# One core, a diffusion block with expert retrieval: left-over dots gather into the ring, the fourth tile's projection moves behind three heads, the first tile's norm moves to the last stage's end

## The chip, the core and the metric

The kernel runs on one core of a Trainium2 chip. Its engines are TensorE (PE in the profile; PEld is its weight load), VectorE (DVE), ScalarE (ACT), GpSimd (POOL) and the queue of SyncE (SP), which here only issues DMAs. GpSimd issues the indirect DMAs (gathers); all transfers run on the same 16 DMA engines. The metric is the device time of one execution in microseconds; lower is better. The median of three runs of the kernel before is 1616.89 us.

## What is computed

One layer of a hybrid block: a mixer (a gated recurrence and a gated linear attention, with an output projection `w_out`), then a retrieval of experts, then a final norm. For this change the second half matters. Each of 512 latent tokens has 8 heads; each head picks 16 of 16,384 experts, so 128 experts a token:

```python
act = jax.nn.gelu(jnp.einsum("td,tkd->tk", xb, u_tab[eb]), approximate=False) * wb
return jnp.einsum("tk,tkd->td", act, v_tab[eb])
...
x = x + mod_l[:, 5] * _peer(u_l, peer_w_q[l], peer_keys[l], peer_u[l], peer_v[l])
return _rmsnorm(x, final_norm_g)
```

`u_tab` and `v_tab` are 16,384 x 1024 floats each. A token needs the dot product of its vector with 128 rows of U, a gelu, and the weighted sum of 128 rows of V.

## The kernel before

The 512 tokens are four tiles of 128: `t0`, `t1` (the list GT) and `d0`, `d1` (the list DT). The two pairs go two ways.

**Gathered tiles (t0, t1).** For each of the 128 experts of a token a gather brings 128 rows of U, one for each token of the tile (128 x 1024 floats), and VectorE forms the dot products of the rows (`u_start` issues the gather, `u_fin` is the dot, L924). After every 16 dots (a head) ScalarE takes the gelu and VectorE multiplies by the weights (`u_done`, L932 and L936). Then 128 gathers of V rows are summed with these weights: for t1 by VectorE (`v_row`, L982), for t0 by TensorE, 128 matmul pairs into the PSUM tile `yv` (`v_pairs`, L973).

**Dense tiles (d0, d1).** The whole U table is streamed in 128 blocks `b` of 128 experts: `d_scores` (L1030) multiplies each block with both tiles, gives 128x256 scores and keeps them, after a gelu, in the three parts of A. The chosen experts' weights are multiplied in by `w_hot`, `w_mm` and `w_mul`. Then the whole V table is streamed (`v_load`, four buffers): `v_split` cuts a block of V and of A into a high and a low part (`vh`, `gh` on ScalarE, `vl`, `gl` on VectorE, L1078 and L1077) and `d_out` (L1090) multiplies gh vh, gh vl and gl vh into `ya`; every sixth block is multiplied unsplit. Blocks 126 and 127 are multiplied at the end, tile by tile, each followed by that tile's `finish`.

**Stages.** (1) The front, to about 402 us: mixer, then for each tile the output projection with its norm (`prep_mm`, 32 matmuls), its transposes (`prep_t`), and the queries and scores of the heads (`q_mm`, `s_mm`). (2) The scores stage, to 910 us: `d_scores` on TensorE; beside it VectorE picks the experts (`select`) and does dots. (3) The weights stage, to 1120 us: `w_*` for the dense tiles and V rows of t0 on TensorE, with 14 dots of t1. (4) The last stage, to the end: `v_split` and `d_out`; beside them the remaining dots of t1 and its 128 V rows (the generator `rest`), then the norms.

**What sets the order.** In stages 2 to 4 the engines run in the order in which the code emits (`manual_schedule`). In the front and stage 2 two generators, `pe_list` and `dve_list`, are merged by two clocks of planned microseconds; a dot of t0 or t1 is put in (`row_u`) whenever VectorE's clock has reached `due`, which then grows by PACE. `done` is a set of marks: "sel" once both dense tiles are picked (before block 100), "end" at block 121, after which no dots are put in, "u" after block 127. In stage 4, after each `d_out(b)`, `rest` is advanced until `want` of its steps are done.

**Buffers.** `ring` has four buffers of 128x1024 floats. Before "sel" every third dot gathers into another tag, `rz`. After "u" a dot gathers into `rw`, which has the tag u_d, two buffers; `vl` has the same tag:

```python
if "u" in done:
    g = B.tile([128, D], F32, name="rw", tag="u_d", bufs=2)
elif "sel" not in done and k % 3 == 2:
    g = zs.tile([128, D], F32, name="rz", bufs=2)
else:
    g = ring()
...
vl = B.tile([128, D], F32R, name="vl", tag="u_d", bufs=2)
```

`finish(t, yt)` is a tile's gated sum and final norm: `fin_rows` loads the gate row and the norm's weights into two ring buffers, `fin_x` the tile's x, and a fourth buffer is scratch. For t0 it stands at the start of stage 4 and reads `yv` in PSUM; t1's stands after block 126.

Of the kernel before, what the change touches and what calls it, by code (L numbers as in the profile page):

```python
# [9 lines left out]
F32 = mybir.dt.float32  # L10
# [10 lines left out]
D = 1024  # L21
# [26 lines left out]
def tile_kernel(ctx, tc, x, cx, pos, ada_w, cols, rows, consts, w_in, wgate, w_g, w_out, w_q, keys_t,  # L48
                peer_u, peer_v, peer_ut, out):
    nc = tc.nc  # L50
    V, S, G, PE, SY = nc.vector, nc.scalar, nc.gpsimd, nc.tensor, nc.sync
# [246 lines left out]
    w = load_in(2464)  # L298
# [325 lines left out]
    for n, k in enumerate((0, 1, 2, 3, 4, 5, 6, 7)):  # L624
        tag, nb = (("acc", 1) if n < 1 else ("wraw", 3) if n < 4 else ("whi", 2) if n < 6 else ("wlo", 2))
        w = wst.tile([128, D], F32, name="wo", tag=tag, bufs=nb)
# [3 lines left out]
    t0, t1 = GT  # L630
    d0, d1 = DT
# [38 lines left out]
    def ring(shape=(128, D), dt=F32):  # L670
        return B.tile(list(shape), dt, name="ring", tag="ring", bufs=RING)
# [10 lines left out]
    def prep_mm(t):  # L682
        xt, pt = xin[t]
        V.tensor_add(xt, xt, pt)
        for n in range(2):
            p = bank("pw")
            for k in range(KD):
                PE.matmul(p, mix_k(k)[:, t * 128:(t + 1) * 128], wo[k][:, n * 512:(n + 1) * 512],
                          start=(k == 0), stop=(k == KD - 1))
            V.tensor_mul(pt[:, n * 512:(n + 1) * 512], p, gate_mix[:, n * 512:(n + 1) * 512])  # L690
        V.tensor_add(xt, xt, pt)
        SY.dma_start(x1_d[t * 128:(t + 1) * 128, :], xt)
        ss = kb.tile([128, 1], F32, name="ss1", bufs=2)
        S.activation(pt, xt, AF.Square, accum_out=ss)
        r = rstd_of(kb, ss, 1, 1.0 / D)
        V.tensor_scalar(pt, xt, r[:, 0:1], None, op0=OP.mult)
# [4 lines left out]
    def prep_t(t):  # L701
        pt = xin[t][1]
        ut = [tok_u(t, k) for k in range(KD)]
        for h in range(2):
            p = bank("pt")
            for j in range(4):
                PE.transpose(p[:, j * 128:(j + 1) * 128], pt[:, (h * 4 + j) * 128:(h * 4 + j + 1) * 128], ident)
            for j in range(4):
                k = h * 4 + j
                if j % 2:  # L710
                    S.activation(ut[k], p[:, j * 128:(j + 1) * 128], AF.Identity,
                                 scale=a2[:, k:k + 1], bias=b2[:, k:k + 1])
                else:
                    V.tensor_scalar(ut[k], p[:, j * 128:(j + 1) * 128], a2[:, k:k + 1], b2[:, k:k + 1],
                                    op0=OP.mult, op1=OP.add)

    def prep_n(t):
        u_n[t] = B.tile([128, D], F32, name=f"u_n{t}")
        for h in range(2):
            p = bank("pu")  # L720
            for j in range(4):
                PE.transpose(p[:, j * 128:(j + 1) * 128], tok_u(t, h * 4 + j), ident)
            S.copy(u_n[t][:, h * 512:(h + 1) * 512], p)
# [129 lines left out]
    L = {}  # L853
# [58 lines left out]
        return g  # L912

    def u_start(t, k):
        if "u" in done:
            g = B.tile([128, D], F32, name="rw", tag="u_d", bufs=2)
        elif "sel" not in done and k % 3 == 2:
            g = zs.tile([128, D], F32, name="rz", bufs=2)
        else:
            g = ring()  # L920
        return t, k, gather(peer_u, sel_i[t][:, k:k + 1], g)
# [33 lines left out]
    yv = []  # L955
# [30 lines left out]
    def fin_rows():  # L986
        fin["gp"] = ring()
        fin["fn"] = ring()
        SY.dma_start(fin["gp"], gp_d)
        SY.dma_start(fin["fn"], row(2))  # L990

    def fin_x(t, g):
        fin[t] = g
        SY.dma_start(g, x1_d[t * 128:(t + 1) * 128, :])

    def finish(t, yt):
        xt, tm = fin[t], ring()
        ss = kb.tile([128, 2], F32, name="ss2", bufs=2)
        for n in range(2):
            c = slice(n * 512, (n + 1) * 512)  # L1000
            V.tensor_mul(tm[:, c], yt(n), fin["gp"][:, c])  # L1001
            V.tensor_add(xt[:, c], xt[:, c], tm[:, c])  # L1002
            S.activation(tm[:, c], xt[:, c], AF.Square, accum_out=ss[:, n:n + 1])  # L1003
        s1 = kb.tile([128, 1], F32, name="ss1", bufs=2)
        V.tensor_add(s1, ss[:, 0:1], ss[:, 1:2])
        r = rstd_of(kb, s1, 1, 1.0 / D)
        for n in range(2):
            c = slice(n * 512, (n + 1) * 512)
            V.scalar_tensor_tensor(xt[:, c], xt[:, c], r[:, 0:1], fin["fn"][:, c], op0=OP.mult, op1=OP.mult)  # L1009
            SY.dma_start(out[t * 128:(t + 1) * 128, c], xt[:, c])  # L1010
# [100 lines left out]
    done = set()  # L1111
# [7 lines left out]
    def pe_list():  # L1119
        prep_mm(t0)  # L1120
        prep_mm(t1)
        yield 28
        prep_mm(d0)
        prep_t(t0)
        prep_t(t1)
        yield 16
        between = {1: lambda: (prep_n(t0), prep_mm(d1)), 3: lambda: prep_t(d0), 4: lambda: prep_n(t1),
                   5: lambda: prep_t(d1)}
        last = None
        for h in range(NH):  # L1130
            for a in (h * 2 + 4, h * 2 + 5):
                if a < 16:
                    wq_load(a)
            q = q_mm(GT, h)
            if last:
                s_mm(*last)
            last = q
            if h in between:
                between[h]()
            yield 22.5 if h == 1 else 8.2  # L1140
        s_mm(*last)
        open_l()
        done.add("l")
        seq = [("u", 0), ("u", 1)]
        for h in range(NH):
            seq += [("w", 2 * h), ("w", 2 * h + 1)] + [("u", 4 * h + 2 + i) for i in range(4)]
        seq += [("u", b) for b in range(34, 128)]
        for n in range(3):
            u_load(*seq[n])
        last = None  # L1150
        region.enter_context(tc.manual_schedule(engines={ET.Activation, ET.PE, ET.DVE, ET.Pool}))
        for n, (kind, b) in enumerate(seq):
            if n + 3 < len(seq):
                u_load(*seq[n + 3])
            if kind == "w":
                if b % 2:
                    if last:
                        s_mm(*last)
                    last = q_mm(DT, b // 2)
                    yield 8.1  # L1160
                continue
            if b == A_PARTS[1]:
                open_a(1)
            if b == A_PARTS[2]:
                while not all(("turn", t) in done for t in DT):
                    yield None
                done.add("sel")
                open_a(2)
            d_scores(b)
            if last and b == 34:  # L1170
                s_mm(*last)
                last = None
            yield 3.45
            if b == 121:
                done.add("end")
        done.add("u")
        flush(True)
        region.close()
# [31 lines left out]
        while "end" not in done:  # L1210
            yield None

    PACE = 2.4
    due = 70.
    ET = mybir.EngineType
    region = ExitStack()
    clock = [0.0, 52.0]
    streams = [pe_list(), dve_list()]
    while streams[0] or streams[1]:
        if "l" in done and "u" not in done:  # L1220
            flush()
        if "end" not in done and clock[1] >= due and clock[1] <= clock[0] + 4 and row_u():
            clock[1] += 1.32
            due = max(due + PACE, clock[1] - 6)
            continue
        i = 0 if streams[0] and (clock[0] <= clock[1] or not streams[1]) else 1
        c = next(streams[i], "end")
        if c == "end":
            streams[i] = None
        elif c is None:  # L1230
            clock[i] = clock[1 - i] + 0.1
        else:
            clock[i] += c
# [25 lines left out]
    if "usage" in globals():  # L1259
        usage("end")  # L1260
    L["y"] = B.tile([128, D], F32, name="y", tag="u_n0")
    fin_rows()
    fin_x(t0, ring())
    finish(t0, lambda n: yv[0][:, n, :])

    def rest():
        for h in range(NH):
# [3 lines left out]
            for _ in range(TOPK):  # L1271
                v_row(t1, left[t1]["v"].pop(0))
                yield

    n_g = len(left[t1]["u"]) + NSEL
    gath = rest()
    k = 0
    with tc.manual_schedule(engines=PIN):
        v_split(0)
        for b in range(128):  # L1280
            if b < 127:
                v_split(b + 1)
            if b + 4 < 128:
                v_load(b + 4)
            elif b < 127:
                fin_x((t1, d0, d1)[b - 124], slot([128, D], "xf"))
            if b < 126:
                d_out(b)
            want = min(n_g, n_g * (b + 1) // 124)
            while k < want:  # L1290
                next(gath, None)
                k += 1
            if b == 124:
                next(gath, None)
                fin_rows()
            if b == 126:
                finish(t1, lambda n: L["y"][:, n * 512:(n + 1) * 512])
        for t in DT:
            for b in (126, 127):
                d_out(b, (t,))  # L1300
            finish(t, lambda n: ya[t][:, n, :])
# [67 lines left out]
```

## Time and profile before

| | |
|---|---|
| runs shown (us) | 1609.41, 1616.89, 1619.64; median 1616.89 |
| profiled execution (us) | 1608.13, of which the span 1606.4 |
| mean granted clock of TensorE | 0.975 of full speed |
| busy, share of the span | PE 93%, PEld 69%, DVE 74%, ACT 33%, POOL 39% |
| matmuls | 6668 |
| stages (us from the span's start) | front to 402, scores to 910, weights to 1120, last to the end |
| moved by DMA | 484.28 MB, mean 301 GB/s |

The busy shares are means over four stages with different limits, so what a change is worth is read stage by stage. A row of a timeline gives start, duration, engine, line, operation, and in brackets the idle time of that engine just before, with what ended it. A busy TensorE is not TensorE at its peak, since matmuls overlap and their ends are modelled.

### The profile page before, as it was taken

The page shows a single profiled execution, that of the slowest core. Times are in us where ns is not written, and L with a number is a line of the kernel's source. Part 1 is how long each engine was busy: PE and PEld are TensorE (multiplying, and loading weights), DVE is VectorE, ACT ScalarE, POOL GpSimd, SP SyncE. Part 2 cuts the span into 40 slices and gives each one's busy share as a digit, 9 for nine tenths or more (in the row PEclk, how much of TensorE's full clock was granted, in tenths as well). Part 3 has the DMA queues.
Part 4 walks back from the last instruction along what each step waited for, and adds up shares of the span by engine and source line. Part 5 has one row for each costly group of instructions (what it writes and reads, how often), then busy time and mean ns, then how long its engine had stood idle before and what let it go on. Part 6 is the DMA issues. An engine that isn't in the chain of part 4 may idle for free. (4 is left out here: it accounts for less than half of the span.)

```text
span 1606.4 us, 20273 instructions
## 1 busy us (share of the span) xinstructions
PE 1486.4 (93%) x6668; PEld 1103.9 (69%) x6668; DVE 1193.9 (74%) x3078; ACT 527.1 (33%) x1001; POOL 630.4 (39%) x579
## 2 busy tenths in 40 slices
PE   8899999999999999999999999999899999696585
PEld 2678778478888888888888744454566667474354
DVE  5889965429989979997964177666788889584467
ACT  3667874122111111111120144444333443232123
POOL 0111100005546646564544376664545555241230
PEclk9999999999999999999999999999999999897798
DMA  9655432448999989998999699999899999795575
GB/s 373 199 183 177 145 118 79 185 152 296 361 359 394 388 324 405 387 399 329 394 371 395 216 347 351 358 348 356 326 359 370 386 369 390 281 332 212 175 258 214
DMA packets 152569, 484.28 MB, mean 301 GB/s; under 512 B 14864, under 2 KB 36752, under 8 KB 152336
## 3 DMA queue, kind: packets, MB, share of 16 engines
q0 software_dynamic: 79072, 287.87, 48.6%
q1 hardware_dynamic: 73392, 195.13, 32.7%
q8 instruction: 52, 0.85, 0.2%
q14 instruction: 53, 0.43, 0.1%
HBM read 477.69 MB, written 5.24 MB: 301 GB/s over the span
## 5 line engine op out<-in xcount | busy, mean ns | idle before, releaser
L910 POOL DMA_INDIRECT ring<-in_dram,sel_i x287 | 363.6, 1267 | 374.8 <-DVE y L982 150.1
L1030 PE MATMUL pds<-u_d,ut_s 128*128 128x256 f32 x2048 | 444.8, 379 | 0.0
L1030 PEld LDWEIGHTS pds<-u_d,ut_s 128*128 128x128 f32 x2048 | 388.4, 190 | 52.5
L924 DVE SCALAR_TENSOR_TENSOR ring<-ring,u_n 128x1024 f32<-128x1024 f32 x159 | 191.8, 1219 | 35.4 <-DMA ring<-in_dram,sel_i 35.3
L1090 PE MATMUL ya<-vl,gh 128*128 128x512 f32 x428 | 146.1, 424 | 63.8 <-DVE vl L1078 63.0
L982 DVE SCALAR_TENSOR_TENSOR y<-ring,act,y 128x1024 f32<-128x1024 f32 x127 | 162.5, 1280 | 28.2 <-DMA ring<-in_dram,sel_i 27.4
L1090 PE MATMUL ya<-vh,gh 128*128 128x512 f32 x428 | 147.5, 427 | 7.1 <-ACT vh L1076 7.1
L1090 PEld LDWEIGHTS ya<-vl,gh 128*128 128x128 f32 x428 | 81.5, 199 | 96.2 <-DVE vl L1078 79.3
L1090 PE MATMUL ya<-vh,gl 128*128 128x512 f32 x428 | 139.7, 409 | 0.0
L1078 DVE TENSOR_TENSOR vl<-vt_s,vh 128x1024 fp32r<-128x1024 f32 x107 | 132.7, 1240 | 9.0 <-ACT vh L1076 8.8
L1033 ACT ACTIVATE A<-pds 128x1024 f32<-128x1024 f32 x32 | 32.8, 1024 | 302.9 <-PE pds L1030 276.9
L1076 ACT CAST vh<-vt_s 128x1024 fp32r<-128x1024 f32 x107 | 112.3, 1049 | 59.3 <-DMA vt_s<-in_dram 47.0
L973 PE MATMUL yv<-ring_s,z 128*64 128x512 f32 x256 | 121.4, 603 | 5.9 <-DMA ring_s<-in_dram,ix 4.0
L973 PE MATMUL yv<-ring,z 128*64 128x512 f32 x256 | 121.5, 603 | 1.2 <-DMA ring<-in_dram,ix 0.7
L1075 ACT CAST gh<-A 128x256 fp32r<-128x256 f32 x107 | 43.4, 405 | 214.7 <-PE ya L1090 192.7
L1090 PEld LDWEIGHTS ya<-vh,gh 128*128 128x128 f32 x428 | 84.2, 198 | 36.9 <-ACT vh L1076 10.0
L910 POOL DMA_INDIRECT rz<-in_dram,sel_i x63 | 76.6, 1215 | 64.0 <-DVE rz L924 37.2
L1090 PEld LDWEIGHTS ya<-vh,gl 128*128 128x128 f32 x428 | 85.0, 199 | 21.1
L924 DVE SCALAR_TENSOR_TENSOR rw<-rw,u_n 128x1024 f32<-128x1024 f32 x34 | 41.6, 1224 | 73.5 <-DMA rw<-in_dram,sel_i 71.5
L1039 DVE TENSOR_TENSOR ab<-cst,sel_t 128x512 f32<-128x512 f32 x64 | 44.1, 689 | 58.7 <-PE pwb L1054 31.8
L910 POOL DMA_INDIRECT ring<-in_dram,ix x64 | 62.8, 982 | 47.9 <-PE pwb L1054 22.1
L910 POOL DMA_INDIRECT ring_s<-in_dram,ix x64 | 63.9, 998 | 44.4 <-DMA ut_s<-in_dram 20.8
(310 smaller groups left out, 2375.5 us busy)
## 6 DMA issues: line engine op xcount, KB each, us to landing
ut_s<-in_dram SPq DMA_DIRECT2D x144, 512.0 KB
vt_s<-in_dram SPq DMA_DIRECT2D x128, 512.0 KB
adw<-in_dram POOLq DMA_DIRECT2D x34, 512.0 KB
wraw<-in_dram SPq DMA_DIRECT2D x21, 512.0 KB
wada<-in_dram SPq DMA_DIRECT2D x16, 512.0 KB
wq<-in_dram SPq DMA_DIRECT2D x16, 512.0 KB
ring<-in_dram,sel_i POOLq DMA_INDIRECT x287
wo<-in_dram SPq DMA_DIRECT2D x8, 512.0 KB
```

The source lines that it names most:

```text
L910: G.indirect_dma_start(out=g, out_offset=None, in_=tab, in_offset=bass.IndirectOffsetOnAxis(ap=ix, axis=0))
L924: V.scalar_tensor_tensor(g, g, 1.0, u_n[t], op0=OP.mult, op1=OP.mult, accum_out=act[t][:, k:k + 1])
L973: PE.matmul(yv[0][h * 64:h * 64 + 64, n, :], z[:, 63 - i:127 - i], g[:, n * 512:(n + 1) * 512], start=(i == 0), stop=(i == 63), skip_group ...
L982: V.scalar_tensor_tensor(L["y"], g, a, L["y"], op0=OP.mult, op1=OP.add)
L1030: PE.matmul(p, ut[:, k], u_d[k // 4][:, k % 4].rearrange("p j t -> p (j t)"), start=(k == 0), stop=(k == KD - 1))
L1033: S.activation(a_of(b - 3, 4), ld["ps"].rearrange("p h n -> p (h n)"), AF.Gelu)
L1039: V.tensor_tensor(ab[:, 0], iota[:, None, :].to_broadcast([128, 4, 128]), st[0][:, j, n0:n0 + 4, None].to_broadcast([128, 4, 128]), op=OP. ...
L1075: S.copy(gh, a)
L1076: S.copy(vh, vt)
L1078: V.tensor_sub(vl, vt, vh.bitcast(F32))
L1090: PE.matmul(ya[t][:, n, :], g[:, j * 128:(j + 1) * 128], v[:, n * 512:(n + 1) * 512], start=(b == 0 and i == 0), stop=(b == 127 and i == l ...
```

## The change

Six edits, all in order and buffers; what is computed stays.

1. `u_start`: with a new mark "w", set when the weights stage has been emitted, dots gather into `ring` instead of `rw`.
2. `between`: the transposes of d0 come after head 0, d1's output projection after head 2 (before: after head 1, and d0's transposes after head 3). The plan's step of 22.5 us moves along.
3. "end" is set at block 124, not 121.
4. After "sel", `due` grows by 2.2, not 2.4.
5. t0's sum is copied from PSUM into `y0` by ScalarE at the start of the last stage; its loads come at block 121 and its `finish` at block 123.
6. `rest` is to be done by block 121, not 124; the gate rows are loaded at 121, not 124; t1's `finish` comes at block 125, not 126.

```diff
     def u_start(t, k):
-        if "u" in done:
+        if "w" in done:
+            g = ring()
+        elif "u" in done:
             g = B.tile([128, D], F32, name="rw", tag="u_d", bufs=2)
...
-        between = {1: lambda: (prep_n(t0), prep_mm(d1)), 3: lambda: prep_t(d0), 4: lambda: prep_n(t1),
+        between = {0: lambda: prep_t(d0), 1: lambda: prep_n(t0), 2: lambda: prep_mm(d1), 4: lambda: prep_n(t1),
                    5: lambda: prep_t(d1)}
...
-            yield 22.5 if h == 1 else 8.2
+            yield 22.5 if h == 2 else 8.2
...
-            if b == 121:
+            if b == 124:
                 done.add("end")
...
-    PACE = 2.4
+    PACE, LATE = 2.4, 2.2
...
-            due = max(due + PACE, clock[1] - 6)
+            due = max(due + (LATE if "sel" in done else PACE), clock[1] - 6)
...
-    fin_rows()
-    fin_x(t0, ring())
-    finish(t0, lambda n: yv[0][:, n, :])
+    y0 = L["abp"].tile([128, D], F32, name="y0")
+    for n in range(2):
+        S.copy(y0[:, n * 512:(n + 1) * 512], yv[0][:, n, :])
...
+    done.add("w")
     n_g = len(left[t1]["u"]) + NSEL
...
-            want = min(n_g, n_g * (b + 1) // 124)
+            want = min(n_g, n_g * (b + 1) // 121)
...
-            if b == 124:
+            if b == 121:
                 next(gath, None)
                 fin_rows()
-            if b == 126:
+                fin_x(t0, ring())
+            if b == 123:
+                finish(t0, lambda n: y0[:, n * 512:(n + 1) * 512])
+            if b == 125:
                 finish(t1, lambda n: L["y"][:, n * 512:(n + 1) * 512])
```

Lines of the changed kernel from `u_start` on are two higher, from the last stage on four to six.

How many dots of t1 stand where follows from the plan. Before, 222 of the 256 dots of both tiles are emitted in the scores stage, 14 in the weights stage and 20 in the last one; of the changed kernel 233, 14 and 9. On VectorE, the end of the last head's dots in the last stage stands like this before (`rw` is the gathered U row, `act` the dots' results, `sel_w` the weights, `y` the sum of V rows):

```order
L1078 TENSOR_TENSOR vl<-vt_s,vh 128x1024
L924 SCALAR_TENSOR_TENSOR rw,act_2318<-rw,u_n_2789 128x1024
L936 TENSOR_TENSOR act_2318<-act_2318,sel_w_2316 128x16
L1077 TENSOR_TENSOR gl<-A_5802,gh 128x256
L1078 TENSOR_TENSOR vl<-vt_s,vh 128x1024
L982 SCALAR_TENSOR_TENSOR y<-ring,act_2318,y 128x1024 x2
```

The same place on VectorE in the changed kernel:

```order
L926 SCALAR_TENSOR_TENSOR ring,act_2318<-ring,u_n_2801 128x1024
L1079 TENSOR_TENSOR gl<-A_5811,gh 128x256
L1080 TENSOR_TENSOR vl<-vt_s,vh 128x1024
L926 SCALAR_TENSOR_TENSOR ring,act_2318<-ring,u_n_2801 128x1024 x3
L938 TENSOR_TENSOR act_2318<-act_2318,sel_w_2316 128x16
L1079 TENSOR_TENSOR gl<-A_5811,gh 128x256
L1080 TENSOR_TENSOR vl<-vt_s,vh 128x1024
L984 SCALAR_TENSOR_TENSOR y<-ring,act_2318,y 128x1024
```

The dots stand between the splits as before, but read the ring, and nine are left of twenty.

On TensorE in the front, the piece of the difference where the heads begin (`pq` are queries, `pss` scores, `pt` transposes of a tile, `pw` the output projection, `pu` transposes for t0's dots):

```order
 L707 MATMUL pt<-cst,p_2323 128x128 x8
-L733 MATMUL pq<-ut_g,wq 128x256 x32
+L733 MATMUL pq<-ut_g,wq 128x256 x16
+L707 MATMUL pt<-cst,ring 128x128 x8
+L733 MATMUL pq<-ut_g,wq 128x256 x16
 L743 MATMUL pss<-kt,q 128x128 x4
 L722 MATMUL pu<-cst,ut_g 128x128 x8
+L733 MATMUL pq<-ut_g,wq 128x256 x16
+L743 MATMUL pss<-kt,q 128x128 x4
 L688 MATMUL pw<-wo,mix_627 128x512 x2
 L688 MATMUL pw<-wo,mix_628 128x512 x2
```

The transposes of d0 stand between the first two heads, and the scores of the second head ahead of the projection.

On VectorE at the end of the last stage, before (`xf` is the tile's x, `ya` the dense sum):

```order
L1077 TENSOR_TENSOR gl<-A_5802,gh 128x256
L1078 TENSOR_TENSOR vl<-vt_s,vh 128x1024
L1077 TENSOR_TENSOR gl<-A_5802,gh 128x256
L1078 TENSOR_TENSOR vl<-vt_s,vh 128x1024
L1001 TENSOR_TENSOR ring<-y,ring 128x512
L1002 TENSOR_TENSOR xf<-xf,ring 128x512
```

And in the changed kernel, from the last row of t1's norm:

```order
L91 TENSOR_TENSOR rs_r<-rs_r,rs_t 128x1
L1011 SCALAR_TENSOR_TENSOR xf<-xf,rs_r,ring 128x512 x2
L1079 TENSOR_TENSOR gl<-A_5811,gh 128x256
L1080 TENSOR_TENSOR vl<-vt_s,vh 128x1024
L1003 TENSOR_TENSOR ring<-ya,ring 128x512
L1004 TENSOR_TENSOR xf<-xf,ring 128x512
```

The split of block 127 stood ahead of t1's norm and now stands behind it; t0's norm stands one split further ahead.

## Rows read from the trace of the kernel before

**Rows 1.** Costliest groups: line, engine, out<-in, count | busy us, mean ns | idle before.
```profile
L1030 PE MATMUL pds<-u_d,ut_s 128*128 128x256 f32 x2048 | 444.8, 379 | 0.0
```
**Rows 2.** Last stage by stretches: length, each engine's busy us, PEclk, DMA share, GB/s.
```profile
1160.00:1380.00 220.00, 210.95 (x816) 151.38 (x815) 195.97 (x207) 86.88 (x120) 108.92 (x87) 1.00 0.99 378
1380.00:1420.00 40.00, 27.40 (x90) 18.89 (x89) 22.54 (x28) 11.27 (x16) 13.39 (x11) 0.83 0.65 231
...
1440.00:1540.00 100.00, 60.71 (x187) 42.27 (x186) 43.19 (x64) 19.24 (x29) 18.88 (x19) 0.81 0.57 198
```
**Rows 3.** Waits from 1120 to 1605: who <- whom: us, times, longest.
```profile
PE ya L1090 <- DVE vl L1078: 63.0, 30, 10.5
...
DVE rw L924 <- DMA rw<-in_dram,sel_i: 70.3, 18, 7.7
DVE y L982 <- DMA ring<-in_dram,sel_i: 27.4, 31, 2.9
```
**Rows 4.** Timeline, one turn of the loop of dots in the last stage.
```profile
1508.94 0.94 POOL L910 DMA_INDIRECT rw<-in_dram,sel_i  x1 [5.38 <-DVE rw L924]
...
1513.82 1.23 DVE L924 SCALAR_TENSOR_TENSOR rw<-rw,u_n 128x1024 f32<-128x1024 f32 x1 [3.62 <-DMA rw<-in_dram,sel_i]
...
1515.30 1.27 DVE L1078 TENSOR_TENSOR vl<-vt_s,vh 128x1024 fp32r<-128x1024 f32 x1
...
1516.63 0.74 PE L1090 MATMUL ya<-vl,gh 128*128 128x512 f32 x2 [0.89 <-DVE vl L1078]
```
**Rows 5.** The same stage by stretches, line L1078 (`vl`) alone: DVE busy us (x).
```profile
1120.00:1160.00 40.00, 11.81 (x10) 0.91 0.88 323
1160.00:1380.00 220.00, 74.08 (x61) 1.00 0.99 378
1380.00:1420.00 40.00, 8.13 (x7) 0.83 0.65 231
...
1440.00:1540.00 100.00, 16.64 (x14) 0.81 0.57 198
```
**Rows 6.** Groups of instructions from 1120 to 1605 us.
```profile
L982 DVE SCALAR_TENSOR_TENSOR y<-ring,act,y 128x1024 f32<-128x1024 f32 x127 | 162.5, 1280 | 28.2 <-DMA ring<-in_dram,sel_i 27.4
...
L1078 DVE TENSOR_TENSOR vl<-vt_s,vh 128x1024 fp32r<-128x1024 f32 x107 | 132.7, 1240 | 9.0 <-ACT vh L1076 8.8
```
**Rows 7.** Scores stage: dots 826 to 878 (groups), stretch 820 to 880, and two timeline rows.
```profile
L924 DVE SCALAR_TENSOR_TENSOR ring<-ring,u_n 128x1024 f32<-128x1024 f32 x24 | 29.4, 1226 | 22.7 <-DMA ring<-in_dram,sel_i 22.7
...
820.00:880.00 60.00, 60.00 (x282) 52.84 (x281) 33.90 (x59) 5.88 (x9) 28.46 (x27) 1.00 0.99 380
...
823.66 86.50 PE L1030 MATMUL pds<-u_d,ut_s 128*128 128x256 f32 x400
...
911.25 1.00 DVE L1062 TENSOR_TENSOR A<-A,pwb 128x112 f32<-128x112 f32 x4 [33.14 <-ACT A L1033]
```
**Rows 8.** Timeline: the same product of two half blocks that follow each other.
```profile
1549.68 0.62 PE L1090 MATMUL ya<-vl,gh 128*128 128x512 f32 x2
...
1551.05 0.63 PE L1090 MATMUL ya<-vl,gh 128*128 128x512 f32 x2
```
**Rows 9.** Timeline, start of the last stage: the first gather of a V row.
```profile
1122.06 0.94 POOL L910 DMA_INDIRECT ring<-in_dram,sel_i  x1 [11.68 <-issue]
```
**Rows 10.** Timeline, end of the last stage.
```profile
1576.48 2.62 DVE L982 SCALAR_TENSOR_TENSOR y<-ring,act,y 128x1024 f32<-128x1024 f32 x2
...
1582.78 0.68 DVE L1001 TENSOR_TENSOR ring<-y,ring 128x512 f32<-128x512 f32 x1
...
1585.55 0.63 ACT L1003 ACTIVATE ring<-xf 128x512 f32<-128x512 f32 x1 [0.60 <-DVE xf L1002]
...
1590.13 0.69 DVE L1001 TENSOR_TENSOR ring<-ya,ring 128x512 f32<-128x512 f32 x1
...
1596.58 0.68 DVE L1001 TENSOR_TENSOR ring<-ya,ring 128x512 f32<-128x512 f32 x1
```
**Rows 11.** Timeline, front: the fourth tile's projection.
```profile
338.37 13.90 PE L688 MATMUL pw<-wo,mix 128*128 128x512 f32 x32
```

## Prediction

> **What bounds the kernel now.** I read the table of costliest groups first. The scores stage (L1030, 2048 matmuls) has no idle time ahead of any of its matmuls [rows 1], so from about 402 to 910 us TensorE alone sets the time, and work that other engines do there is free as long as TensorE stays fed. Next the table by stretches for the last stage, 1120 us to the end. In the 220 us from 1160 to 1380 TensorE is busy 211 us and the DMA engines are at 0.99 with 378 GB/s; in 1380 to 1420 and 1440 to 1540 the DMA share is 0.65 and 0.57, TensorE is busy 27 of 40 and 61 of 100 us, and its granted clock is 0.83 and 0.81, a mix of the 2.4 and the 1.2 GHz level [rows 2]. There nothing is full, so something waits. The waits say what: TensorE waits 63.0 us for `vl` (30 waits), and VectorE waits 70.3 us, in 18 waits, for the gathers of `rw`; its 31 waits for gathers of V rows come to 27.4 [rows 3]. The timeline shows one turn of that loop: the gather of a dot's U row starts only when the dot before it has freed its buffer (5.38 us idle on GpSimd), the dot starts 4.9 us later, the `vl` of the next block of experts stands behind the dot on VectorE, and TensorE waits for that `vl` [rows 4]. `rw` and `vl` share the two buffers of tag u_d, so a gather can never run far ahead. Twenty dots stand in this stage.
>
> **The pace beside the stall.** `vl` is made for five blocks of six and takes 1.240 us [rows 6], so busy time of that line counts blocks. 1160 to 1380: 74.08 / 1.240 x 6/5 = 71.7 blocks [rows 5], 3.07 us each. The two slow stretches: (8.13 + 16.64) / 1.240 x 6/5 = 24.0 blocks in 140 us; at 3.07 they would take 73.6, so the stall costs 66.4 us. The first 40 us: 11.4 blocks, 35.1 at that pace, so the start loses 4.9.
>
> **The change part by part.**
>
> *Left-over dots in the ring, and fewer of them.* The emitted order of the changed kernel leaves 9 dots in the last stage, in groups of 2, 1, 1, 1, 1 and 3; 11 moved into the scores stage. The nine gather into the four-buffer ring that the V rows use, so they are requested as early as V rows are, and hold no `vl` buffer. A dot takes 1.23 us, a V row 1.28 [rows 4, 6]: on VectorE a dot is a V row. What is left is the end of the group: three dots in a row, and the gelu on ScalarE behind the last one, before the next `gh` and `vh`. I take 3.5 us for it; its bounds are 0 (hidden) and nine waits like today's, 9 x 70.3/20 = 31.6. **Gain 62.9.**
>
> *The eleven moved dots.* They lengthen the train of dots in the scores stage. From 826 to 878 us 24 dots run at 52/24 = 2.17 us each, held by their gathers, then VectorE idles 33.14 us until the last gelu of that stage [rows 7]. Eleven more need 11 x 2.17 = 24 us, to about 902, less what is gained by an earlier beginning. They fit in the idle time: cost 0. Were that cover gone they would cost their 24 us. They also keep the DMA engines full there; in 820 to 880 the share is 0.99 and TensorE is busy all 60 us [rows 7], so full queues do not starve it. The gathers for the first V pairs stand behind the dots on GpSimd's queue, and may come up to a few us late for TensorE at 910. I take 0, bound 5.
>
> *The pace.* Each gather and each load is 128 rows of 4 KB, 0.524 MB. Before, 20 dots and 128 V rows lie over 124 blocks: (1 + 148/124) x 0.524 = 1.150 MB a block, at 378 GB/s 3.04 us, which is the pace found (3.07): the steady stretch is held by transfers. After, 137 over 121 blocks: 1.118 MB, 2.96 us. Bounds: 3.07 (no gain), and TensorE's own rate. Two weight sets of one half block start 1.37 us apart [rows 8], so a split block takes 2.74; with the unsplit sixth a little above, 2.81. Blocks until the last V row: 124 x 3.07 = 380.7 before, 121 x 2.96 = 358.2 after. **Gain 22.5**, of which three blocks are only moved into the tail below.
>
> The Trainium skill (DMA: Bandwidth & Descriptors, Specifications) gives about 358 GB/s as the HBM limit of one core. By that rule a block of 1.118 MB would take 3.12 us and this gain would shrink by 19. The trace does not agree: it holds 378 over 220 us [rows 2]. The sum goes by the trace.
>
> *First tile's norm moved to the end.* At the start of the stage it goes: six VectorE passes of about 0.7 us, a ScalarE round, and three loads into the ring, behind which the first gather stood 11.68 us [rows 9]. In its place two ScalarE copies of 128x512 out of PSUM stand ahead of the first `vh`. No such copy is in the trace; the nearest, a 0.63 us pass of the norm [rows 10], gives 1.3 us at most, as long as the wait for VectorE there now. Of the 4.9 lost I take **gain 4** (0 to 5).
>
> At the end it comes back. Today, after the last V row (over at 1579.10), come two `vl`, the second tile's norm (1582.78 to 1590.13), the third's (6.45, to 1596.58), and the fourth's with its output, 9.8 to the end at 1606.4: 27.3 us in all [rows 10]. In the new VectorE order three `gl`, `vl` pairs (4.8 us), the first tile's norm (7.4, with the table load), one pair (1.6), the second tile's norm (6.45) and one more pair (1.6) follow the last V row: 21.9. Behind it TensorE still has to use that last `vl` (1.3, half a block), then come the third tile's norm (6.45) and the fourth's with its output (9.8): 39.4. **Loss 12.1.** So the last split of V stands behind two norms on VectorE, and what is late next is TensorE's block 127, for which the third tile's norm waits.
>
> *Fourth tile's projection behind three heads.* The same matmuls in another order: 13.9 us of projection change places with a head's queries and the third tile's transposes. VectorE's first selection can go on about 14 us sooner, since it waits for the second head's scores, which stand behind the projection today [rows 11]. TensorE has no wait to lose here. Value 0 for TensorE; the time goes into dots, already counted. The later `end` (124 for 121) and the pace of 2.2 for 2.4 are counted there too.
>
> **Sum**, against the profiled execution (span 1606.4, 1608.1 in all): -62.9 - 22.5 - 4 + 12.1 = -77.3, so 1530.8. The median of the runs shown is 1616.9, 8.8 above this execution. The same gain from there is 1539.6; I forecast **1540**.
>
> **The rivals.**
> *The dots still wait.* The ring also carries the V rows, and on full queues a gather may take as long as today. For it: in the scores stage ring dots wait 22.7 us over 24 [rows 7]. Against: that is 0.95 each, not 3.5. At 31.6 instead of 3.5: 1568.
> *The pace stays.* TensorE and VectorE are both near full at 3.07 (211 and 196 of 220 us [rows 2]), so fewer bytes may buy nothing, or the transfers may slow down once the pauses of the stall are gone: 121 x 0.11 = 13 us lost, 1553; with a gather late at 910 (5), 1558. (The rule of the skill's page above would put the time in this case, at 1540 + 121 x 0.16 = 1559.)
> *The pace falls to TensorE's rate.* With the loop gone and VectorE lighter: 121 x 0.15 = 18 us more, 1522.
> *Scores stage starved (slower).* With queues full to about 902, `ut_s` comes late at each block from 813 on, TensorE's clock falls to the 1.2 GHz level as in the stall now, and a block costs 6.92 instead of 3.46 (86.5 us for 25 blocks [rows 7]). All 28 blocks would cost 97 us, net 1637; it decides from 23 such blocks on (77/3.46). Against: the stretch 820 to 880 is already as full, with TensorE never idle.
> *No effect.* If dots were not the cause: no, their waits are in the trace.
>
> **How the numbers follow.** Forecast 0.68, dots still wait 0.13, pace stays 0.08, TensorE's rate 0.07, starved 0.03, no effect 0.01. The range reaches from TensorE's rate with the lower base (1522 - 6) to the waiting dots: **1515 to 1570**. About 1% is what this kernel's runs can tell. Every case but the last two is faster by more: faster 0.96, same 0.02, slower 0.02.
>
> **What would show it.** Right: no wait of VectorE for `rw` in the last stage, under 15 us of waits of TensorE for `vl`, nine ring dots, DMA share near 1 up to the last V row, dots in the scores stage until about 900 with TensorE still gapless, and about 39 us from the last V row to the end. Wrong: a DMA share near 0.6 around the nine dots (they still wait), an unchanged count of blocks per 100 us (pace stays), idle time before L1032 (starved), or a tail far from 39 us (the norms' term).

## The result, and the profile after

The changed kernel takes 1533.11 us (median of four runs, 1527.17 to 1534.41) where the kernel before takes 1616.02 beside it: a ratio of 0.9484, with a 95% interval from 0.9444 to 0.9524. The forecast was 1540, range 1515 to 1570. The profiled execution has a span of 1530.3 us, 76.1 less than the 1606.4 before; the sum of the prediction said 77.3.

The page of the changed kernel first: busy time by engine, the slices of TensorE's clock and of the DMA share (40 equal slices of the span, each digit in tenths; 9 is 90% or more), and the groups that answer to [rows 1] and [rows 6].

```profile
span 1530.3 us, 20260 instructions
...
PE 1472.1 (96%) x6668; PEld 1100.5 (72%) x6668; DVE 1192.9 (78%) x3078; ACT 529.4 (35%) x1003; POOL 653.9 (43%) x579
...
PEclk9999999999999999999999999999999999999997
DMA  9655522626999999999999989999999999999993
...
L1032 PE MATMUL pds<-u_d,ut_s 128*128 128x256 f32 x2048 | 445.0, 379 | 0.0
...
L984 DVE SCALAR_TENSOR_TENSOR y<-ring,act,y 128x1024 f32<-128x1024 f32 x127 | 162.5, 1279 | 18.6 <-DMA ring<-in_dram,sel_i 17.9
```

VectorE's busy time is that of before within a few us; what went is idle time. The scores stage is still without a gap on TensorE (0.0). From that stage on the clock is at 9 and the DMA share at 8 or more in every slice but the last. Before there were two holes, [rows 2]; the same stretches after:

```profile
1160.00:1380.00 220.00, 215.58 (x839) 156.51 (x838) 195.58 (x207) 89.58 (x123) 114.97 (x84) 1.00 0.98 377
1380.00:1420.00 40.00, 38.80 (x154) 28.42 (x153) 35.18 (x39) 16.02 (x22) 22.59 (x15) 1.00 1.00 387
1440.00:1480.00 40.00, 39.13 (x155) 28.69 (x154) 35.89 (x42) 15.77 (x24) 20.64 (x16) 1.00 0.98 376
```

Every stretch now looks like the undisturbed one: TensorE near full at a granted clock of 1.00, DMA share 0.98 to 1.00. `vl` alone (columns as in [rows 5]) counts the blocks:

```profile
1160.00:1490.00 330.00, 113.71 (x93) 1.00 0.99 377
```

113.71 us at 1.232 each (the mean of its group in this stage) are 92.3 splits, times 6/5 110.8 blocks, in 330 us: 2.98 us a block, now with the nine dots in it. The waits of TensorE and of VectorE from 1120 to 1530 us, to lay beside [rows 3]:

```profile
PE ya L1092 <- DVE vl L1080: 10.6, 17, 1.8
PE ya L1092 <- ACT vh L1078: 6.6, 3, 4.1
...
DVE vl L1080 <- ACT vh L1078: 18.1, 19, 6.1
DVE y L984 <- DMA ring<-in_dram,sel_i: 17.9, 21, 2.8
```

No row names `rw` any more, and TensorE waits 10.6 us for `vl` instead of 63.0. The nine dots themselves, from the view of their line in this stage (count, duration min/median/max, first and last start; then what their engine waited for):

```profile
L926 DVE SCALAR_TENSOR_TENSOR ring<-ring,u_n x9: 1211/1218/1226, 1424.5 to 1444.5; 128x1024 f32<-128x1024 f32 x9
...
  DMA ring<-in_dram,sel_i: 1.4, 2
```

1.4 us of waiting for nine dots, where twenty had waited 70.3.

The time splits at three points: the first product of the last stage on TensorE, the start of the last V row on VectorE, and the end.

| us from the span's start | scores stage | last product of `yv` | first product of `ya` | last V row | end | first `ya` to last V row | last V row over to end |
|---|---|---|---|---|---|---|---|
| before | 402.0 to 909.8 | 1119.1 | 1120.1 | 1577.8 | 1606.4 | 457.7 | 27.3 |
| changed | 403.7 to 912.9 | 1122.4 | 1125.1 | 1487.2 | 1530.3 | 362.1 | 41.8 |

So the stage up to the last V row gave 95.6, the tail took back 14.5, and the stage began 5.0 later: together 76.1.

### The profile page after: what moved, and what is told of

Its sections match the earlier page's. It is cut to its first block, busy times and chain, and to the rows that moved or that the text cites. A ratio compares the mean times of both kernels' runs of the same rounds, so it can differ in the third digit from the quotient of the medians.

```text
span 1530.3 us, 20260 instructions
## 1 busy us (share of the span) xinstructions
PE 1472.1 (96%) x6668; PEld 1100.5 (72%) x6668; DVE 1192.9 (78%) x3078; ACT 529.4 (35%) x1003; POOL 653.9 (43%) x579
## 4 chain that ended last, share of the span: by engine, by line
PE 71%; DMA 11%; issue 7%; DVE 5%; ACT 3%; POOL 2%; SPq 0%; DVEq 0%; POOLq 0%; ACTq 0%
PE pds L1032 29%; PE ya L1092 10%; PE yv L975 7%; PE pq L733 7%; DMA ring<-in_dram,sel_i 6%; PE pwb L1056 4%; PE pw L688 4%; POOL ring L910 2%; DMA wada<-in_dram 2%; PE pa L279 1%; PE pa L276 1%; PE pa L277 1%; DMA adw<-in_dram 1%; DVE vl L1080 1%; PE pss L743 1%
## 5 line engine op out<-in xcount | busy, mean ns | idle before, releaser
L910 POOL DMA_INDIRECT ring<-in_dram,sel_i x306 | 401.7, 1313 | 503.2 <-DVE eq L837 155.9
L926 DVE SCALAR_TENSOR_TENSOR ring<-ring,u_n 128x1024 f32<-128x1024 f32 x178 | 214.8, 1218 | 49.6 <-DMA ring<-in_dram,sel_i 49.5
L1092 PE MATMUL ya<-vh,gh 128*128 128x512 f32 x428 | 143.2, 416 | 6.6 <-ACT vh L1078 6.6
L1092 PE MATMUL ya<-vl,gh 128*128 128x512 f32 x428 | 138.4, 405 | 10.6 <-DVE vl L1080 10.6
L1092 PE MATMUL ya<-vh,gl 128*128 128x512 f32 x428 | 134.1, 395 | 0.0
L1078 ACT CAST vh<-vt_s 128x1024 fp32r<-128x1024 f32 x107 | 112.4, 1051 | 38.7 <-DMA vt_s<-in_dram 33.9
L910 POOL DMA_INDIRECT rz<-in_dram,sel_i x64 | 80.9, 1264 | 63.3 <-DVE rz L926 39.9
L1092 PEld LDWEIGHTS ya<-vh,gl 128*128 128x128 f32 x428 | 81.3, 190 | 20.0
L1056 PEld LDWEIGHTS pwb<-ab 128*128 128x128 f32 x512 | 61.4, 194 | 28.8 <-issue 24.9
L926 DVE SCALAR_TENSOR_TENSOR rz<-rz,u_n 128x1024 f32<-128x1024 f32 x64 | 77.7, 1214 | 0.5 <-issue 0.3
```

The costliest lines, as they stand in the source:

```text
L910: G.indirect_dma_start(out=g, out_offset=None, in_=tab, in_offset=bass.IndirectOffsetOnAxis(ap=ix, axis=0))
L926: V.scalar_tensor_tensor(g, g, 1.0, u_n[t], op0=OP.mult, op1=OP.mult, accum_out=act[t][:, k:k + 1])
L1056: PE.matmul(p[:, n * 128:(n + 1) * 128], ab[:, 1, n], ab[:, 0, n], start=True, stop=True)
L1078: S.copy(vh, vt)
L1092: PE.matmul(ya[t][:, n, :], g[:, j * 128:(j + 1) * 128], v[:, n * 512:(n + 1) * 512], start=(b == 0 and i == 0), stop=(b == 127 and i == l ...
```

## The experiments

The experiments stand in three groups; each group ran on one chip, beside the kernel before. There were three chips, and the kernel before took 1595.4, 1615.6 and 1593.6 us on them, so ratios to the kernel before are compared, not times. The changed kernel's own ratio came out at 0.9484 (above), 0.9467 and 0.9501; a thousandth is 1.6 us.

**Edit 1 alone**, in the kernel before, with all its twenty dots:

```diff
-        if "u" in done:
+        if "w" in done:
+            g = ring()
+        elif "u" in done:
...
+    done.add("w")
     n_g = len(left[t1]["u"]) + NSEL
```

> The kernel before with edit 1 alone: its 20 dots of the last stage gather into the ring; every other edit is left out, so the plan, the norms and the number of dots stay. Theory (the gathers of dots waited for the two buffers that vl holds as well): the 66 us of stall nearly vanish, the pace stays 3.04 to 3.07 us a block, so 1617 - 60 = about 1557. Rival (ring dots wait as long as today, since V rows fill the ring): still over 1600.

Ratio 0.9546 (0.9524 to 0.9568): 4.5% of the 5.2% come from the buffer alone, some 73 us. VectorE's waits from 1101 to 1490 us:

```profile
DVE y L984 <- DMA ring<-in_dram,sel_i: 22.0, 29, 1.9
...
DVE ring L926 <- DMA ring<-in_dram,sel_i: 4.7, 5, 1.2
```

Twenty ring dots wait 4.7 us, and the part from the first product to the last V row falls from 457.7 to 387.0, 3.12 us for each of 124 blocks. The stall is gone as a whole, and it was worth more than the 60 us expected here: the part is 70.7 us shorter. The rival, that ring dots wait as long as `rw` dots, falls.

**The changed kernel without edit 1**: its nine dots gather into `rw`.

```diff
-        if "w" in done:
-            g = ring()
-        elif "u" in done:
+        if "u" in done:
             g = B.tile([128, D], F32, name="rw", tag="u_d", bufs=2)
```

> The changed kernel without edit 1: its nine dots of the last stage gather into rw again. Theory: nine of twenty dots bring back nine twentieths of the stall, 9 x 3.3 = 30 us, so about 1563, with waits of VectorE for rw near 9 x 3.5 = 32 us. Rival (the gain comes from moving eleven dots and spreading the rest, not from the buffer): about 1540.

Ratio 0.968 (0.966 to 0.9701), that is 29 to 34 us more than the changed kernel. Its waits of VectorE, two stretches (columns as in [rows 2]) and two dots of its timeline:

```profile
DVE rw L924 <- DMA rw<-in_dram,sel_i: 29.5, 9, 6.5
```

```profile
1160.00:1380.00 220.00, 215.19 (x840) 156.92 (x839) 197.27 (x211) 88.52 (x122) 127.97 (x85) 1.00 0.99 378
1380.00:1480.00 100.00, 80.05 (x279) 56.78 (x278) 65.42 (x79) 29.75 (x43) 30.32 (x28) 0.90 0.76 275
```

```profile
1431.60 1.23 DVE L924 SCALAR_TENSOR_TENSOR rw<-rw,u_n 128x1024 f32<-128x1024 f32 x1 [3.52 <-DMA rw<-in_dram,sel_i]
1437.80 1.23 DVE L924 SCALAR_TENSOR_TENSOR rw<-rw,u_n 128x1024 f32<-128x1024 f32 x1 [3.44 <-DMA rw<-in_dram,sel_i]
```

Nine dots wait 29.5 us, 3.3 each, and the hole is back around them: DMA share 0.76, clock 0.90. A dot that shares its buffers with `vl` costs the stage 3.3 to 3.5 us (29.5 / 9 here, 70.3 / 20 before), whichever of the other edits are there. This run and the one before meet from both sides, so the cause is shown: it is the buffer. What it is about the buffer is not separated. Edit 1 takes the dots from two buffers to four and away from `vl` at once, and no run gives them two buffers of their own. In the kernel before, GpSimd holds back gathers of `rw` for both reasons, more for the first:

```profile
POOL rw L910 <- DVE rw L924: 58.1, 11, 6.2
...
POOL rw L910 <- PE ya L1090: 15.5, 6, 4.4
```

It waits 58.1 us for the dot ahead to free its buffer, and 15.5 us for TensorE to be done with a `vl`.

**The changed kernel without edits 3 and 4** (`end` at 121, pace 2.4), so that 16 dots are left for the last stage:

```diff
-            if b == 124:
+            if b == 121:
                 done.add("end")
...
-    PACE, LATE = 2.4, 2.2
+    PACE, LATE = 2.4, 2.4
```

> The changed kernel without edits 3 and 4 (end at block 121, pace 2.4): 226 dots in the scores stage, 14 in the weights stage, 16 in the last one, in the ring. Theory (the last stage is held by transfers): seven more gathers of 0.524 MB at 378 GB/s, 7 x 1.39 = 9.7 us, so about 1543. Rival (TensorE or VectorE holds the pace, or the gathers moved into the scores stage cost as much there): 1531 to 1536.

Ratio 0.9537 (0.9512 to 0.9563): 6 to 11 us more than the changed kernel by its three ratios, though the interval overlaps two of theirs, and against those two 3 us or less are not excluded. The 9.7 of the theory lie in that range, but the profile does not show them. From the first product to the last V row it takes 364.2 us with 16 dots; the three profiles of the changed kernel take 362.1 to 365.3 with nine, the next run 360.8 with eleven. The transfers make up for the seven gathers:

```profile
1160.00:1380.00 220.00, 214.63 (x833) 155.17 (x832) 200.20 (x212) 88.14 (x122) 122.10 (x89) 1.00 1.00 386
```

They move 386 GB/s where the changed kernel's three profiles have 370 to 377, so the price of 1.39 us a gather, taken at 378 GB/s, is not shown. The profiled execution is the fastest of six (1515.7 to 1528.5 us). What edits 3 and 4 are worth stays open.

**The changed kernel without edit 2** (the front in its old order; eleven dots left):

```diff
-        between = {0: lambda: prep_t(d0), 1: lambda: prep_n(t0), 2: lambda: prep_mm(d1), 4: lambda: prep_n(t1),
+        between = {1: lambda: (prep_n(t0), prep_mm(d1)), 3: lambda: prep_t(d0), 4: lambda: prep_n(t1),
...
-            yield 22.5 if h == 2 else 8.2
+            yield 22.5 if h == 1 else 8.2
```

> The changed kernel without edit 2 (the front in the order of before); two more dots are then left for the last stage, 11 in all. Theory (the front order moves nothing that TensorE waits for, it only gives VectorE time): 2 x 1.39 = 3 us, so about 1536. Rival (the order itself saves the 14 us that a projection lasts): about 1547. Second rival (the new order costs TensorE time in the front): 1530 or less.

Ratio 0.9498 (0.9475 to 0.9521), which cannot be told from the changed kernel. 14 us for the order itself are excluded. Whether its two dots are worth 3 us is below what these runs resolve. The scores stage begins at 403.2 us here and at 403.7 to 405.1 in the three profiles of the changed kernel.

**The changed kernel without edits 5 and 6**: the first tile's norm at the start of the stage again, gathers spread to block 124, the second tile's norm after block 126. The changed kernel ran beside it.

```diff
-    y0 = L["abp"].tile([128, D], F32, name="y0")
-    for n in range(2):
-        S.copy(y0[:, n * 512:(n + 1) * 512], yv[0][:, n, :])
+    fin_rows()
+    fin_x(t0, ring())
+    finish(t0, lambda n: yv[0][:, n, :])
...
-            want = min(n_g, n_g * (b + 1) // 121)
+            want = min(n_g, n_g * (b + 1) // 124)
...
-            if b == 121:
+            if b == 124:
                 next(gath, None)
                 fin_rows()
-                fin_x(t0, ring())
-            if b == 123:
-                finish(t0, lambda n: y0[:, n * 512:(n + 1) * 512])
-            if b == 125:
+            if b == 126:
                 finish(t1, lambda n: L["y"][:, n * 512:(n + 1) * 512])
```

> The changed kernel itself, beside the kernels of this call, as their measure. All theories: 0.948 of the kernel before.

> The changed kernel without edits 5 and 6: the first tile's norm at the start of the last stage, gathers spread to block 124, the second tile's norm after block 126; the nine ring dots and the plan stay. Theory (the norm costs more at the end, 41.8 - 27.3 = 14.5 us of tail, than it loses at the start, 3, and the three blocks won by block 121, 3 x 2.98 less 1.4 for the thinner gathers, do not make up for it): about 4 us faster than the changed kernel. Rival (the move is worth what was lost at the start and more): 4 us slower or more.

Ratios 0.9467 (0.9447 to 0.9487) for the changed kernel and 0.9472 (0.9454 to 0.9491) without the two edits: no difference. The profiles show the exchange. With the norm at the start, the part up to the last V row takes 373.4 us for 124 blocks, in the changed kernel 365.3 for 121; the tail is 26.5 against 41.9. The tail's 15.4 us buy 8.1 there; in the medians the two kernels are 2.6 us apart, inside their spreads; the profiled executions are the slowest of five for the changed kernel and the fastest of five for this one. The 4 us faster that were expected were not seen, and neither was the rival's gain of 4 or more.

**Half of the second tile's V rows not gathered**, while VectorE, ScalarE and TensorE do all their work (the row before is added twice; GpSimd issues fewer gathers):

```diff
-        g = gather(peer_v, sel_i[t][:, k:k + 1], ring())
+        if k % 2 == 0:
+            L["g"] = gather(peer_v, sel_i[t][:, k:k + 1], ring())
+        g = L["g"]
```

> The changed kernel with every second V row of the second tile not gathered: the row before it is added again, so VectorE, ScalarE and TensorE do what they did and 64 of 137 gathers of the last stage are left out (the output is not the reference's for that tile). Theory (transfers hold the pace of the last stage): a block falls from 2.98 us to TensorE's own 2.81, so 121 x 0.17 = 20 us faster than the changed kernel. Rival (TensorE or VectorE holds it): within 5 us of the changed kernel.

Ratio 0.9421 (0.9407 to 0.9435): 1522.27 us where the changed kernel beside it takes 1531.88. The stretch from 1160 to 1440 us of this kernel:

```profile
1160.00:1440.00 280.00, 278.64 (x1093) 204.96 (x1092) 255.77 (x279) 115.09 (x160) 79.69 (x60) 1.00 0.85 289
```

and of the changed kernel on the same chip:

```profile
1160.00:1440.00 280.00, 273.29 (x1057) 196.82 (x1056) 247.48 (x269) 111.67 (x155) 152.88 (x106) 1.00 0.98 373
```

With fewer transfers TensorE is busy 278.6 of 280 us and the DMA share falls to 0.85; the part up to the last V row takes 351.0 instead of 365.3, 2.90 us a block instead of 3.02. So both readings are half right. Transfers do hold the changed kernel's pace, but TensorE's own rate lies only 0.12 us below it, not 0.17. Of the 20 us expected, 14.3 appear in this part and 9.6 in the median.

**The two early norms one split later** (first tile's after block 125, second's after 126), to free TensorE's last blocks:

```diff
-            if b == 123:
+            if b == 125:
                 finish(t0, lambda n: y0[:, n * 512:(n + 1) * 512])
-            if b == 125:
+            if b == 126:
                 finish(t1, lambda n: L["y"][:, n * 512:(n + 1) * 512])
```

> The changed kernel with the first tile's norm after block 125 and the second's after block 126, so that the splits of blocks 126 and 127 each stand one norm further ahead on VectorE. Theory (in the tail TensorE waits 7.3 us for splits that stand behind two norms): TensorE's waits go, and the tail falls from 41.8 to VectorE's own chain, four splits of 1.6 and norms of 7.4, 6.5, 6.5 and 9.8, together 36.6: 5 us faster. Rival (the norms in a row on VectorE set the tail whatever their order): no difference over 2 us.

Ratio 0.9474 (0.9457 to 0.9491) beside 0.9467: the rival was right. In its timeline TensorE's waits in the tail are down, but VectorE goes from norm to norm:

```profile
1498.35 0.68 DVE L1003 TENSOR_TENSOR ring<-y,ring 128x512 f32<-128x512 f32 x1
...
1504.65 0.73 PE L1092 MATMUL ya<-vh,gh 128*128 128x512 f32 x2 [1.19 <-ACT vh L1078]
...
1507.17 0.68 DVE L1003 TENSOR_TENSOR ring<-y,ring 128x512 f32<-128x512 f32 x1
1507.30 0.74 PE L1092 MATMUL ya<-vl,gh 128*128 128x512 f32 x2 [1.92 <-DVE vl L1080]
...
1513.61 0.69 DVE L1003 TENSOR_TENSOR ring<-ya,ring 128x512 f32<-128x512 f32 x1
...
1520.06 0.68 DVE L1003 TENSOR_TENSOR ring<-ya,ring 128x512 f32<-128x512 f32 x1
```

TensorE waits 3.1 us in these two places. VectorE begins a norm at 1498.35, 1507.17, 1513.61 and 1520.06, without a wait ahead of any. The tail is 41.0 us, not 36.6. Five splits of 1.6 stand in it, not the four of the expectation, and VectorE waits 3.1 us between them before the first norm, for TensorE (1.35) and for ScalarE's `vh` (1.76).

**Each early norm in two halves** behind successive splits (the first tile's after blocks 122 and 123, the second's after 125 and 126), beside the changed kernel on the third chip:

```diff
-            if b == 123:
-                finish(t0, lambda n: y0[:, n * 512:(n + 1) * 512])
-            if b == 125:
-                finish(t1, lambda n: L["y"][:, n * 512:(n + 1) * 512])
+            if b == 122:
+                half = finish_a(t0, lambda n: y0[:, n * 512:(n + 1) * 512])
+            if b == 123:
+                finish_b(t0, half)
+            if b == 125:
+                half = finish_a(t1, lambda n: L["y"][:, n * 512:(n + 1) * 512])
+            if b == 126:
+                finish_b(t1, half)
```

> The changed kernel itself once more, as the measure for the three kernels of this call. All theories: 0.947 to 0.948 of the kernel before.

> The changed kernel with each of the two early norms in two halves: the first tile's after blocks 122 and 123, the second's after 125 and 126, each half behind a split. Theory (in the tail VectorE is the chain; it idles some 4.6 us between the splits, waiting for TensorE, before the first norm, and 2 us within each norm for ScalarE): the first half fits into that idle time, tail 37 instead of 41.9 us, 4 to 5 us faster. Rival (the tail is set by TensorE's last blocks, which a norm earlier holds up as much): within 2 us of the changed kernel.

Ratios 0.9501 (0.9479 to 0.9524) for the changed kernel and 0.9492 (0.9467 to 0.9517) for this one. The tail falls from 41.7 to 40.3, not to 37, and the medians are 2.3 us apart inside their spreads: closer to the rival than to the theory. The first half now waits for its own load:

```profile
1472.41 0.69 DVE L1007 TENSOR_TENSOR ring<-ring 128x512 f32<-128x512 f32 x1 [1.92 <-DMA ring<-x_d]
...
1475.52 0.43 DVE L1086 TENSOR_TENSOR gl<-A,gh 128x256 fp32r<-128x256 f32 x1 [1.08 <-ACT gh L1084]
```

and the next split waits behind the norm's squares on ScalarE.

**The nine dots into the weights stage** (23 there, none in the last), and **all of it together** with `end` at 127 (239 dots in the scores stage, 17 in the weights stage) and the norms in halves:

```diff
-                g = n < 30 and u_next(t1)
+                g = n < 48 and u_next(t1)
```

> The changed kernel with the limit of dots in the weights stage raised, so that its last nine dots stand there (23 in all) and none in the last stage. Theory (the last stage is held by transfers down to TensorE's own rate, and the weights stage has 378 - 345 = 33 GB/s over 205 us = 6.8 MB to spare for nine gathers of 0.524 MB, 4.7 MB): the last stage comes near the 351 us up to its last V row of the run with half the V rows, so 9 to 12 us faster than the changed kernel. Rival (in the weights stage the dots hold up the gathers for TensorE on GpSimd's queue, or VectorE): the 12 us come back there, within 3 us of the changed kernel.

> The two edits of the runs above together, and end set at block 127, so that 239 dots stand in the scores stage, 17 in the weights stage and none in the last one. Theory (the three add up): 14 to 17 us faster than the changed kernel. Rival (the dots of the last three blocks of the scores stage hold up the first V pairs): no faster than the better one of the two.

Ratios 0.9517 (0.9492 to 0.9542) and 0.9484 (0.946 to 0.9509), beside 0.9501: neither can be told from the changed kernel. The time moves back a stage. With 23 dots the last stage up to its last V row takes 356.2 us instead of 363.7. From the end of the scores stage to the last product of `yv` it takes 197.8 instead of 191.2: 7.5 won, 6.6 lost. For the whole bundle it is 9.6 won, 8.6 lost. The weights stage from 920 to 1100 us, of the changed kernel and then of the one with 23 dots:

```profile
920.00:1100.00 180.00, 178.89 (x950) 91.72 (x950) 137.09 (x416) 94.22 (x297) 130.51 (x132) 1.00 1.00 383
```

```profile
920.00:1100.00 180.00, 177.76 (x909) 87.20 (x906) 143.42 (x421) 89.84 (x287) 135.50 (x136) 1.00 1.01 395
```

On this chip the stage had little to spare: 383 GB/s and a share of 1.00 without the nine dots, and 395 with them, 12 more and not 33. The room that I had counted came from a trace with 345 GB/s there.

## Why the prediction was right, point by point

*The sum.* That 76.1 us stand against 77.3 is in part luck. Up to the last V row the terms add up to 62.9 + 22.5 + 4 = 89.4, and 95.6 were gained; the tail lost 14.5 and not 12.1, and the stage began 5.0 later, which the sum had at nothing. The errors cancel. Most of the first is in the account of the kernel before: 380.7 + 66.4 + 4.9 = 452.0 where the part takes 457.7, because the stall was counted in two stretches only (1380 to 1420 and 1440 to 1540 us) and the time around them was left out.

*The stall.* Right in cause; the term was too small. Edit 1 alone brings some 73 us, 70.7 of them in this part, where the term was 62.9. The nine dots in `rw` cost 29 to 34, with 31.6 as their price. The residue of 3.5 us was too much: TensorE is busy 39.1 of 40 us right around the end of the dots.

*The pace.* 2.98 us a block against the 2.96 predicted. The whole part, 121 x 2.96 + 3.5 of residue + 0.9 lost at the start = 362.6, came out at 362.1. The bound below it was wrong: TensorE's own rate is 2.90, not 2.81, as the run with half the V rows shows. The unsplit block was priced too low: 2.81 allows it some 3.2 us, and in that run's trace it takes 3.4 (from 1315.12 to 1318.15 us, and 0.4 more in the pair behind it). The rival of TensorE's rate could not have given 1522 from there: 121 x (2.96 - 2.90) is 7 us, not 18. The Trainium skill (DMA: Bandwidth & Descriptors, Specifications) gives about 358 GB/s as one core's limit; the runs do not agree, with 373 to 387 GB/s in stretches of this stage and 395 in a weights stage.

*The moved dots.* They cost TensorE no wait, as said. The last dot of the scores stage begins at 893.06, earlier than the 902 predicted, and VectorE then idles 20.11 us:

```profile
893.06 1.23 DVE L926 SCALAR_TENSOR_TENSOR ring<-ring,u_n 128x1024 f32<-128x1024 f32 x1 [0.55 <-DMA ring<-in_dram,sel_i]
...
914.40 0.70 DVE L1064 TENSOR_TENSOR A<-A,pwb 128x112 f32<-128x112 f32 x2 [20.11 <-ACT A L1035]
```

*The norm at the end.* The tail is 41.8 us, not 39.4; 14.5 lost instead of 12.1. Rows of the tail:

```profile
1494.89 0.69 DVE L1003 TENSOR_TENSOR ring<-y,ring 128x512 f32<-128x512 f32 x1
...
1503.85 0.74 PE L1092 MATMUL ya<-vl,gh 128*128 128x512 f32 x2 [1.80 <-DVE vl L1080]
...
1509.12 1.22 PE L1092 MATMUL ya<-vh,gh 128*128 128x512 f32 x2 [4.07 <-ACT vh L1078]
...
1512.79 1.05 PE L1092 MATMUL ya<-vh,gl 128*128 128x512 f32 x2
...
1513.88 0.69 DVE L1003 TENSOR_TENSOR ring<-ya,ring 128x512 f32<-128x512 f32 x1 [2.17 <-PE ya L1092]
...
1517.89 0.64 PE L1092 MATMUL ya<-vh,gl 128*128 128x512 f32 x2
```

The split of block 127 stands behind two norms, as predicted, and TensorE waits 1.80, 4.07 and 1.43 us for splits. From the last V row's end (1488.51) to the end of that split (1511.71) it is 23.2 us, predicted 21.9: VectorE had small waits between the splits ahead of the first norm that the sum left out. Then the third tile's norm waits 2.17 us for TensorE, predicted 1.3: after its wait of 4.07 us a pair of matmuls takes 1.22 and 1.05 us where it takes 0.62 at the full level, so the last blocks ran at 1.2 instead of 2.4 GHz until 1517.89. From 1502 to 1509 us TensorE is busy 1.25 of 7 us, and from 1509 to 1518 its granted clock is 0.51. (The Trainium skill, TensorE: Matmul & The Clock Gate, Part 1, says that the array falls to half clock when it idles; the rows agree.) I had priced that half block at the full level. The last two norms took 16.4, predicted 16.3.

*The start.* I took 4 us for the norm's leaving. The two copies out of PSUM delay the first `vh`, which VectorE waits 6.1 us for, and TensorE begins 2.7 us after the last product of `yv` instead of 1.0. The count that the prediction used is the busy time of `vl` in the first 40 us:

```profile
1120.00:1160.00 40.00, 13.22 (x11) 0.96 0.93 339
```

By it, 13.22 us instead of 11.81 [rows 5] are 12.9 blocks instead of 11.4, so that 1.6 us are lost there and not 4.9, which is near the term. The run without edits 5 and 6 does not bear that out: its part differs by 8.1 us for three blocks more, which at 2.98 us each leaves nothing for the start. What this step alone is worth stays open; the exchange of the two edits is worth nothing that was measured. In the prediction too it came to nearly nothing: 4 and three blocks of 2.96 against 12.1.

*The front.* No term, and none found. The later beginning of the stage, 5.0 us, is made up so: 1.7 lie ahead of the scores stage, whose start moves between 402.0 and 406.0 over all profiles with either front order; 1.4 in the scores stage, which now holds one pair of the V products (1.07 us, at 905.13); 0.2 in the weights stage; and 1.7 are the copies.

*Against the median* the forecast was 7 us too high, since the measured gain of the medians is 82.9 and that of the profiled executions 76.1; the sum was made for the latter.

## What to carry to other kernels

A transfer that is requested into a buffer which the consumer's own product also needs was a loop here, not a prefetch: look for a wait that repeats with the same releaser, price it by its count, and give the transfer a tag that runs ahead. Once that hole was closed, this stage stood at two limits some 0.1 us a block apart, and work moved to a neighbouring stage with queues as full only moved the time. Work moved into a tail bought nothing here, since the engine that does it is the tail's own chain.

## What the runs showed of the hardware that was not expected

The weights stage, which no edit of the change touches, takes a different time on different chips: 207 to 210 us from the end of the scores stage to the last product of `yv` in the profiles of before, of the changed kernel and of the second group, 188 to 195 in the first group's four kernels and 191 for the changed kernel in the third. That is about the 20 us by which the kernel before differs between the chips. The changed kernel on the second chip (the third is above, with 383 GB/s):

```profile
920.00:1100.00 180.00, 169.75 (x871) 85.89 (x872) 125.42 (x380) 79.72 (x270) 119.77 (x120) 0.97 0.97 351
```

Fewer matmuls in the same time, at 351 GB/s. The rate is 8% lower than on the third chip and the DMA share only 3%, 0.97 for 1.00. That points to transfers that take longer there more than to transfers that are asked for later, but neither was tried, and the cause stays open. A term that rests on spare transfers in one trace should be read on a second chip first.
